# Scale of the first norm from small TensorE products with the weight blocks as stationary operand, loaded in blocks of 128 columns

## Chip, cores and metric

The kernel runs on one core of one Trainium2 chip. The metric is the device time of one execution in microseconds (us); the median of the runs is compared. Before the change three runs took 1184.43, 1188.86 and 1189.87 us, median 1188.86.

## What is computed

One decoder layer on 1024 tokens of width 1024, in float32. What matters here is the first line of the layer: a norm whose scale and shift come from a vector `c`.

```python
c_act = jax.nn.silu(c)
mod = c_act @ w_mod[l] + b_mod[l]
sh1, sc1, g1, sh2, sc2, g2 = jnp.split(mod[:, None, :], N_MOD, axis=-1)
h = rms_norm(x, norm_mix_w[l]) * (1.0 + sc1) + sh1
proj = h @ w_in[l]
```

`w_mod` is 1024 x 6144, so `sc1` alone is the product of a vector with a 1024 x 1024 matrix of 4 MB. After `proj` come a gated recurrence and a gated delta rule (which inverts triangular 128 x 128 blocks), an output projection, and a multi-layer perceptron with a norm of the same kind.

## The kernel before, in words

**Recorder and planner.** The body does not issue instructions. `Proxy` and `Queue` objects stand for the engines (PE is TensorE, V or DVE VectorE, A or ACT ScalarE, G or POOL GpSimd, SP the DMA queue) and record each operation with a modelled length. `Recorder.schedule` (lines 176 to 319) then runs a greedy list schedule over the engines and `emit` (line 321) issues the operations in that order from line 329, which is why nearly every row of the profile reads L329. Each engine then works through its own list strictly in that order. The planner's numbers are at the top: `LAT` (lines 40 to 42), `COLD` (before that time TensorE operations are counted twice, line 286), and the length of a DMA, bytes over 358 per ns (line 408). Operations recorded with `rec.bb` are TensorE's backbone; others are fitted around it.

**The beginning.** `x` comes as eight tiles `xt` of 128 tokens. `xnorm(t)` squares one on ScalarE, takes the reciprocal root on GpSimd (`rs`) and scales it on VectorE (tile 3 on ScalarE). `xhalf(hf, k)` transposes four 128 x 128 blocks on TensorE into one PSUM tile `xTp`, and makes from it the high part `hh` (ScalarE) and the remainder `hl` (VectorE) of the normed and scaled activations, both multiplied by column `k` of `A1`, the scale. `hf` 0 covers tokens 0 to 511, `hf` 1 the others. So nothing can be projected before `A1`.

**A1 before.** The weights of `sc1` come in eight loads `sc1_w`, four for columns 0 to 511 and four for 512 to 1023, in runs of 512 columns (2 KB). `sc1_part` (line 704) adds the eight row blocks, each times its element of `cact` (the column of silu(c)), into `sc1_acc`: blocks 1, 3 and 5 of each half are multiplied on ScalarE and added on GpSimd (`SC1_POOL`), the others go through VectorE. Four products with a column of ones (`sc1_c`, line 722) sum over the partitions, and two VectorE operations make four columns of `A1`.

**After A1.** `Proj.split` (line 642) splits a 1024 x 128 block of `w_in` into `wh` (ScalarE) and `wl` (GpSimd). `Proj.third(i)` multiplies a third of the tokens: 8 blocks by 3 matmuls of 342 columns into `p`. The order on TensorE is the first third of `k0`, of `ab` (`ab_third`, 16 matmuls) and of `k1` (lines 745 to 748), the transposes of `hf` 1, the second thirds, then the column sums `sh_c` of the shift (`sh1_acc`, lines 752 to 757, added up from eight 512 KB loads `sh1_w`), which everything after needs as two further columns of `hh` and `hl`; then `ab`'s last third. From it follow `gcs`, `gT`, a round trip to DRAM (`gdr`, `k_gb`), the decay `k_dm`, and for each of four heads `key(h)`: `ktok`, `kk`, `LT`. When `LT` of all four is there, `inverse` (line 887) does a long VectorE recurrence (`ftmp`, `xx`) and the TensorE products `ie`, `ig`, `ih`, `ix`. TensorE works on `z`, `q` and `v` projections beside it.

**Loads.** All DMAs go through one queue, SP, in its order: `c`, x0, x1, three small ones, x2, x3, four `sc1_w`, the block of `w_in` for `k0`, `wab`, four `sc1_w`, x4, x5, the block for `k1`, x6, x7, two small ones, eight `sh1_w`, eight small rows. Each waits for the landing of the one eight places before it. The eight small rows end in `rows_ps`, a transposition on TensorE (line 741).

Of the kernel before, what the change touches and what calls it, by code (L numbers as in the profile page):

```python
# [10 lines left out]
F32 = mybir.dt.float32  # L11
F32R = mybir.dt.float32r
AF = mybir.ActivationFunctionType
ALU = mybir.AluOpType
# [5 lines left out]
P = 128  # L20
T = 1024
D = 1024
NK = 8
# [8 lines left out]
COL_X, COL_Y, COL_Q, COL_K, COL_V, COL_Z, COL_AB = 0, 512, 1024, 1536, 2048, 2560, 3072  # L32
# [7 lines left out]
LAT = {("PE", "DVE"): 0.2, ("PE", "ACT"): 0.2, ("ACT", "DVE"): 0.04, ("DVE", "ACT"): 0.04, ("ACT", "POOL"): 0.08,  # L40
       ("DVE", "POOL"): 0.08, ("POOL", "DVE"): 0.04, ("POOL", "ACT"): 0.04, ("DVE", "PE"): 0.06, ("ACT", "PE"): 0.06,
       ("POOL", "PE"): 0.06, ("DVE", "DVE"): 0.04, ("ACT", "ACT"): 0.04, ("POOL", "POOL"): 0.05, ("PE", "PE"): 0.0}
SC1_EARLY = 4
SC1_POOL = (1, 3, 5)
COLD = 30.0
SIDE_SCALE = 1.4
TINY_RUN, TINY_SHARE = 0.2, 1.0
SLACK, SLACK_TINY = 0.3, 2.0
# [78 lines left out]
class Recorder:  # L127
# [48 lines left out]
    def schedule(self):  # L176
# [34 lines left out]
        while done < len(ops):  # L211
# [72 lines left out]
            else:  # L284
                t = max(t, port) if op.port else t
                now[e] = fin = t + op.dur * (2 if e == "PE" and t < COLD else 1)
                port = max(port, fin) if op.port else port
# [51 lines left out]
class Proxy:  # L339
# [5 lines left out]
    def __getattr__(self, name):  # L345
        fn = getattr(self.nce, name)

        def call(*a, **k):
            isap = lambda v: isinstance(v, (View, bass.AP))
            outs = [v for n, v in k.items() if n in ("out", "accum_out") and isap(v)]  # L350
            rest = list(a)
            if "out" not in k:
                outs.append(rest.pop(0))
            ins = [v for v in rest if isap(v)] + [v for n, v in k.items() if n not in ("out", "accum_out") and isap(v)]
            self.rec.add(self.eng, fn, a, k, outs, ins, self.length(name, outs[0], ins, k), self.port(name, outs[0], ins))
            return None
        return call
# [39 lines left out]
class Queue(Proxy):  # L397


    def __getattr__(self, name):  # L400
        fn = getattr(self.nce, name)

        def call(out, in_):
            n = 4
            big_ = out if isinstance(out, View) else in_
            for d in big_.shape:
                n *= d
            self.rec.add("SP", fn, (), {"out": out, "in_": in_}, [out], [in_], 0.05 + n / 358e3)
            self.rec.ops[-1].load = isinstance(out, View)
        return call  # L410

# [2 lines left out]
def hybrid_body(ctx, tc, x, c, norm_mix_w, norm_mlp_w, w_mod, b_mod, w_in,  # L414
# [3 lines left out]
                w_out, w_up, w_down, final_norm_w, out, dbg=None):  # L418
    nc = tc.nc
    rec = Recorder(nc)  # L420
    PE, V, A, G = (Proxy(rec, n, e) for n, e in (("PE", nc.tensor), ("DVE", nc.vector), ("ACT", nc.scalar), ("POOL", nc.gpsimd)))
    SP = Queue(rec, "SP", nc.sync)
# [16 lines left out]
    def buf(pool, tag, bufs, shape, dt, name):  # L439
        key = (tuple(shape), dt)  # L440
        if key not in protos:
            protos[key] = dp.tile(list(shape), dt, tag=f"proto{len(protos)}", name=f"proto{len(protos)}")
        b = Buf(pool, tag, bufs, tuple(shape), dt, name, protos[key])
        return View(b, protos[key])

    def big(name, dt=F32, n=1024):
        return buf(bp, "b", N_B, [P, n], dt, name)
# [7 lines left out]
    def ps(name):  # L455
        return buf(pp, "ps", N_PS, [P, 512], F32, name)

    def small(name, n, dt=F32):
        return buf(cp, name, 1, [P, n], dt, name)

    def v3(ap, n=128):
        return ap.rearrange("p (a b) -> p a b", b=n)
# [8 lines left out]
    def mm(o, lhsT, rhs, start=True, stop=True, **kw):  # L471
        PE.matmul(o, lhsT, rhs, start=start, stop=stop, **kw)

    def tr(o, in_, idn):
        PE.transpose(o, in_, idn)
# [11 lines left out]
    ones = small("ones", P)  # L487
# [15 lines left out]
    ccol, cth, cact = small("ccol", 8), small("cth", 8), small("cact", 8)  # L503
# [15 lines left out]
    bcol = small("bcol", 64)  # L519
# [25 lines left out]
    wm_r = w_mod.rearrange("a (k p) n -> (a k) p n", p=P)  # L545
    halves = [slice(0, 512), slice(512, 1024)]

    def macc(acc, wt, k, spread=False):
        if k == 0:
            if spread:  # L550
                A.mul(acc, wt, cact[:, 0:1])
            else:
                V.tensor_scalar(acc, wt, cact[:, 0:1], None, op0=ALU.mult)
        elif spread:
            A.mul(wt, wt, cact[:, k:k + 1])
            G.tensor_tensor(out=acc, in0=acc, in1=wt, op=ALU.add)
        else:
            V.scalar_tensor_tensor(out=acc, in0=wt, scalar=cact[:, k:k + 1], in1=acc, op0=ALU.mult, op1=ALU.add)

# [2 lines left out]
    def load_w(c0, name):  # L562
        w = big(f"{name}_w")
        SP.dma_start(out=v3(w), in_=wr_[:, :, c0:c0 + P])
        return w
# [13 lines left out]
    sc1_w, sh1_w = {}, {}  # L579
    wm_p = w_mod.rearrange("a (k p) n -> (a p) k n", p=P)  # L580
    rec.early = True
    for t in range(4):
        SP.dma_start(out=xt[t], in_=xs[t])
        if t == 1:
            SP.dma_start(out=rows2[0:48, :], in_=b_mod.rearrange("a (r p) -> (a r) p", p=P))
            SP.dma_start(out=rows2[48:56, :], in_=norm_mix_w.rearrange("a (r p) -> (a r) p", p=P))
            SP.dma_start(out=rows2[56:64, :], in_=norm_mlp_w.rearrange("a (r p) -> (a r) p", p=P))
    for n in range(4):
        sc1_w[n] = big(f"sc1_w{n}")
        SP.dma_start(out=v3(sc1_w[n], 512), in_=wm_p[:, 2 * n:2 * n + 2, D:D + 512])  # L590
    wk0 = load_w(COL_K, "k0")
    wab = big("wab")[:, 0:64].rearrange("p (k j) -> p k j", j=8)
    SP.dma_start(out=wab, in_=wr_[:, :, COL_AB:COL_AB + 8])
    for n in range(4):
        sc1_w[4 + n] = big(f"sc1_w{4 + n}")
        SP.dma_start(out=v3(sc1_w[4 + n], 512), in_=wm_p[:, 2 * n:2 * n + 2, D + 512:2 * D])
    for t in range(4, NT):
        if t == 6:
            wk1 = load_w(COL_K + P, "k1")
        SP.dma_start(out=xt[t], in_=xs[t])  # L600
    rec.early = False

# [4 lines left out]
    A1 = small("A1", NK)  # L607
# [28 lines left out]
    class Proj:  # L636
# [2 lines left out]
            self.b = None  # L639
            self.p = {}  # L640

        def split(self):
            raw = self.raw or load_w(self.c0, self.name)
            self.w = (big(f"{self.name}_wh", F32R), big(f"{self.name}_wl", F32R))
            A.copy(self.w[0], raw)
            G.tensor_tensor(out=self.w[1], in0=raw, in1=self.w[0].bitcast(F32), op=ALU.subtract)

        def third(self, i):
            self.p[i] = p = ps(f"{self.name}_p{i}")
# [18 lines left out]
    projs = [Proj(COL_K, "k0", True, wk0), Proj(COL_K + P, "k1", True, wk1)]  # L668
# [17 lines left out]
    def xhalf(hf, k):  # L686
        px = ps(f"xTp{k}_{hf}")
        for j in range(4):
            tr(px[:, j * P:(j + 1) * P], xt[4 * hf + j][:, k * P:(k + 1) * P], ident)
        a, b = hT[k]  # L690
        s = halves[hf]
        A.activation(a[:, s], px, AF.Identity, scale=A1[:, k:k + 1])
        V.scalar_tensor_tensor(out=b[:, s], in0=px, scalar=A1[:, k:k + 1], in1=a[:, s].bitcast(F32),
                               op0=ALU.mult, op1=ALU.subtract)
# [4 lines left out]
    pt = ps("rows2_ps")  # L699
    tr(pt[:, 0:64], rows2, ident[:64, :64])  # L700
    V.tensor_copy(bcol, pt[:, 0:64])
    sc1_acc = big("sc1_acc")

    def sc1_part(hf, ks):
        acc = sc1_acc[:, halves[hf]]
        wts = [sc1_w[4 * hf + k // 2][:, halves[k % 2]] for k in range(NK)]
        for k in ks:
            if k in SC1_POOL:
                A.mul(wts[k], wts[k], cact[:, k:k + 1])
                if k != SC1_POOL[0]:  # L710
                    G.tensor_tensor(out=wts[SC1_POOL[0]], in0=wts[SC1_POOL[0]], in1=wts[k], op=ALU.add)
            else:
                macc(acc, wts[k], k)
        if 7 in ks and SC1_POOL:
            V.tensor_tensor(out=acc, in0=acc, in1=wts[SC1_POOL[0]], op=ALU.add)

    sc1_part(0, range(8))
    for hf in range(2):
        pc = ps(f"sc1_c{hf}")
        ks = slice(4 * hf, 4 * hf + 4)  # L720
        for k in range(4):
            mm(pc[:, 4 * hf + k:4 * hf + k + 1], sc1_acc[:, (4 * hf + k) * P:(4 * hf + k + 1) * P], ones[:, 0:1])
        V.tensor_tensor(out=A1[:, ks], in0=pc[:, ks], in1=bcol[:, 8 + ks.start:8 + ks.stop], op=ALU.add)
        V.scalar_tensor_tensor(out=A1[:, ks], in0=A1[:, ks], scalar=1.0, in1=bcol[:, 48 + ks.start:48 + ks.stop],
                               op0=ALU.add, op1=ALU.mult)
        if hf == 0:
            projs[0].split()
            sc1_part(1, range(SC1_EARLY))
        for k in range(4 * hf, 4 * hf + 4):
            xhalf(0, k)  # L730
        if hf == 0:
            sc1_part(1, range(SC1_EARLY, 8))
    for t in range(4, NT):
        xnorm(t)
    for k in range(NK):
# [8 lines left out]
    rec.bb = True  # L744
    projs[0].third(0)
    ab_third(0)
    projs[1].split()
    projs[1].third(0)
    rec.bb = False
    for k in range(NK):  # L750
        xhalf(1, k)
    sh1_acc = big("sh1_acc")
    for k in range(NK):
        macc(sh1_acc, sh1_w[k], k, k < 3)
    psh = ps("sh1_c")
    for k in range(NK):
        mm(psh[:, k:k + 1], sh1_acc[:, k * P:(k + 1) * P], ones[:, 0:1])
# [28 lines left out]
    for t in range(NT):  # L786
# [7 lines left out]
                    in1=dtb[:, None, :].to_broadcast([P, 8, 4]), op=ALU.add)  # L794
# [137 lines left out]
    def mod_part(vec, name, acc, k):  # L932
        wt = big(f"{name}_w{k}")
        SP.dma_start(out=wt, in_=wm_r[k, :, vec * D:(vec + 1) * D])
        macc(acc, wt, k, k == 0)

    def mod_sum(vec, name):
        acc = big(f"{name}_acc")
# [355 lines left out]
    for t in range(NT):  # L1294
        for i in range(2):
            gemm_o(lcat, lw, t, i, f"wl{t}{i}",
                   lambda p, s: V.scalar_tensor_tensor(out=x1[t][:, s], in0=p, scalar=rsl[:, t:t + 1], in1=x1[t][:, s],
                                                       op0=ALU.mult, op1=ALU.add))
# [300 lines left out]
```

## Time and profile before

| what | value |
|---|---|
| runs | 1184.43, 1188.86, 1189.87 us, median 1188.86 |
| the profiled execution: its own time | 1189.07 us |
| its span, first to last instruction | 1187.2 us |
| TensorE busy in the span | 1142.0 us, 96% |
| VectorE, ScalarE, GpSimd busy | 857.9, 617.3, 385.8 us |
| mean granted TensorE clock | 0.980 of full speed |
| moved by DMA | 229.52 MB, 193 GB/s over the span |

A row of a timeline reads: start, length, engine, operation, what it writes and reads, count, and in brackets how long its engine was idle before and what ended that. PEld is TensorE's loading of the stationary operand, PE its matmuls. A chain of waits is followed back from the last instruction: each row is the work, or the wait, that held up what comes next. A table by stretches gives for each stretch the busy time of every engine, the granted clock, and the DMA's busy share and rate. The granted clock is shown as 1.00 until the first change of it in an execution.

### The profile page before, as it was taken

How to read it: one execution, taken by the hardware profiler on the slowest of the kernel's cores; microseconds unless marked ns; L12 is line 12 of the kernel's file. 1: busy time of each engine (PE TensorE's matmuls, PEld its weight loads, DVE VectorE, ACT ScalarE, POOL GpSimd, SP SyncE). 2: the span in 40 equal slices, each digit the busy share in tenths (PEclk: the TensorE clock that was granted, in tenths of full speed). 3: DMA queues.
4: the chain of work that ended last, by engine and by line, in shares of the span. 5: the costliest groups of instructions: out<-in, count | busy, mean ns of one | idle time of the engine just before them, and what ended most of it. 6: DMA issues, size and time to landing. Idle time of an engine off the chain costs nothing.

```text
span 1187.2 us, 15989 instructions
## 1 busy us (share of the span) xinstructions
PE 1142.0 (96%) x5936; PEld 989.2 (83%) x5936; DVE 857.9 (72%) x1125; ACT 617.3 (52%) x990; POOL 385.8 (32%) x229
## 2 busy tenths in 40 slices
PE   3999899999999999999999999999999999999997
PEld 3889899999999997877888888888788888888885
DVE  6968696698987899977966666656775578775553
ACT  6547317435453868367665555555655524443341
POOL 4708620335242563400001121121430076822130
PEclk7899998999989999999999999999999999999999
DMA  9622430623651635323067777866899848855531
GB/s 338 206 74 101 147 124 19 212 72 115 224 195 54 199 124 210 107 107 107 36 231 256 246 264 241 273 230 235 302 401 387 314 160 312 302 206 188 197 147 71
DMA packets 127151, 229.52 MB, mean 193 GB/s; under 512 B 10657, under 2 KB 51806, under 8 KB 127074
## 3 DMA queue, kind: packets, MB, share of 16 engines
q1 hardware_dynamic: 127074, 228.51, 55.8%
q8 instruction: 46, 0.75, 0.3%
q14 instruction: 31, 0.25, 0.1%
HBM read 171.83 MB, written 56.65 MB: 192 GB/s over the span
## 4 chain that ended last, share of the span: by engine, by line
PE 84%; DVE 7%; issue 3%; ACT 2%; POOL 1%; DMA 1%; SPq 1%; POOLq 0%; DVEq 0%; ACTq 0%
PE dn L329 26%; PE upx L329 15%; PE upz L329 7%; PE k_p L329 4%; PE wg L329 4%; PE upy L329 4%; PE lx_p L329 3%; PE v_p L329 3%; PE ly_p L329 3%; PE wl L329 3%; PE q_p L329 2%; PE ch L329 2%; DVE xx L329 1%; DVE ftmp L329 1%; DMA x<-in_x_dram 1%
## 5 line engine op out<-in xcount | busy, mean ns | idle before, releaser
L329 PE MATMUL upx<-h2h,U 128*128 128x512 f32 x512 | 167.8, 394 | 0.0
L329 POOL TENSOR_TENSOR wd<-wd,wd 128x512 f32<-128x512 f32 x32 | 44.7, 1400 | 231.3 <-DMA wd<-in_w_down_dram 214.4
L329 PEld LDWEIGHTS upx<-h2h,U 128*128 128x128 f32 x512 | 96.1, 188 | 22.7 <-issue 0.2
L329 PE MATMUL upx<-h2l,U 128*128 128x512 f32 x256 | 100.9, 394 | 0.0
L329 ACT ACTIVATE act<-act 128x512 f32<-128x512 f32 x112 | 70.6, 633 | 38.6 <-DVE act L329 37.2
L329 DVE TENSOR_TENSOR U<-wu,U 128x512 fp32r<-128x512 f32 x112 | 76.7, 704 | 16.6 <-ACT U L329 16.5
L329 PE MATMUL upz<-h2h,U 128*128 128x512 f32 x256 | 85.0, 394 | 0.0
L329 ACT CAST U<-wu 128x512 fp32r<-128x512 f32 x112 | 67.2, 618 | 18.4 <-DVE wu L329 9.1
L329 DVE TENSOR_TENSOR act<-upz,ek 128x512 f32<-128x512 f32 x32 | 22.1, 691 | 60.3 <-PE upz L329 44.9
L329 ACT COPY ek<-upx 128x512 f32<-128x512 f32 x48 | 28.1, 586 | 59.7 <-PE upx L329 59.5
L329 PEld LDWEIGHTS upx<-h2l,U 128*128 128x128 f32 x256 | 48.1, 188 | 11.4
L329 PEld LDWEIGHTS upz<-h2h,U 128*128 128x128 f32 x256 | 48.1, 188 | 11.2
L329 POOL TENSOR_TENSOR xb<-xb,keep 128x512 f32<-128x512 f32 x8 | 13.5, 1696 | 122.8 <-DVE keep L329 122.8
L329 PE MATMUL upz<-h2l,U 128*128 128x512 f32 x128 | 50.3, 393 | 0.0
L329 PE MATMUL upy<-h2h,U 128*128 128x512 f32 x128 | 42.7, 394 | 0.0
L329 ACT ACTIVATE vn<-ch,bcoef 128x128 f32<-128x128 f32 x32 | 11.6, 367 | 57.0 <-PE ch L329 57.0
L329 POOL TENSOR_TENSOR ssq<-ssq,mhalf 128x1 f32<-128x1 f32 x16 | 11.7, 732 | 90.0 <-DVE ssq L329 89.9
L329 PE MATMUL k_p<-hh,k_wh 128*128 128x342 f32 x96 | 32.3, 337 | 5.0 <-DVE hl L329 3.9
L329 PE MATMUL z_p<-hh,z_wl 128*128 128x342 f32 x96 | 31.5, 328 | 3.2 <-POOL z_wl L329 3.2
L329 PE MATMUL k_p<-hl,k_wh 128*128 128x342 f32 x96 | 32.7, 341 | 0.0
L329 DVE TENSOR_TENSOR wu<-wu,wu 128x512 f32<-128x512 f32 x48 | 32.6, 683 | 0.0
L329 PE MATMUL k_p<-hh,k_wl 128*128 128x342 f32 x96 | 32.2, 335 | 0.0
(572 smaller groups left out, 3788.2 us busy)
## 6 DMA issues: line engine op xcount, KB each, us to landing
L<-aod SPq DMA_DIRECT2D x56, 512.0 KB, 4.7
R<-in_w_down_dram SPq DMA_DIRECT2D x40, 512.0 KB, 6.6
wu<-in_w_up_dram SPq DMA_DIRECT2D x32, 512.0 KB, 4.2
aod<-as SPq DMA_DIRECT2D x64, 256.0 KB, 3.0
wd<-in_w_down_dram SPq DMA_DIRECT2D x32, 512.0 KB, 7.2
aod<-act SPq DMA_DIRECT2D x48, 256.0 KB, 2.6
x<-in_x_dram SPq DMA_DIRECT2D x16, 512.0 KB, 4.8
sc_w<-in_w_mod_dram SPq DMA_DIRECT2D x16, 512.0 KB, 5.8
```

The costliest lines, as they stand in the source:

```text
L329: op.fn(*[res(v) for v in op.a], **{n: res(v) for n, v in op.k.items()})
```

## The change

`sc1` is made wholly on TensorE. Its weights are loaded in eight blocks of 128 columns, `sc1_w[j]`, each with all eight row blocks; their runs are 512 bytes. For each `j` eight products accumulate one column in PSUM: the stationary operand is a 128 x 128 block of weights, the moving one a single column of `cact`. One VectorE operation turns it into a column of `A1`, with the bias and the norm's weight folded into `B1` ahead of it, and `xhalf(0, j)` follows at once. The multiplications and additions of `sc1_part` are gone from VectorE, ScalarE and GpSimd. The first two weight splits go from GpSimd to VectorE. In the loads, the block for `k1` and `wab` move ahead of x4. The sum of `sh1` loses its GpSimd share: one multiplication on ScalarE, seven operations on VectorE. Two numbers of the planner change, and with them its order everywhere.

```diff
-SC1_EARLY = 4
-SC1_POOL = (1, 3, 5)
-COLD = 30.0
+COLD = 11.0
...
-            self.rec.add("SP", fn, (), {"out": out, "in_": in_}, [out], [in_], 0.05 + n / 358e3)
+            self.rec.add("SP", fn, (), {"out": out, "in_": in_}, [out], [in_], 0.05 + n / 390e3)
...
-    for n in range(4):
-        sc1_w[n] = big(f"sc1_w{n}")
-        SP.dma_start(out=v3(sc1_w[n], 512), in_=wm_p[:, 2 * n:2 * n + 2, D:D + 512])
+    def load_sc1(j):
+        sc1_w[j] = v3(big(f"sc1_w{j}"))
+        SP.dma_start(out=sc1_w[j], in_=wm_p[:, :, D + j * P:D + (j + 1) * P])
+
+    for j in range(4):
+        load_sc1(j)
     wk0 = load_w(COL_K, "k0")
+    for j in range(4, NK):
+        load_sc1(j)
+    wk1 = load_w(COL_K + P, "k1")
     wab = big("wab")[:, 0:64].rearrange("p (k j) -> p k j", j=8)
     SP.dma_start(out=wab, in_=wr_[:, :, COL_AB:COL_AB + 8])
-    for n in range(4):
-        sc1_w[4 + n] = big(f"sc1_w{4 + n}")
-        SP.dma_start(out=v3(sc1_w[4 + n], 512), in_=wm_p[:, 2 * n:2 * n + 2, D + 512:2 * D])
     for t in range(4, NT):
-        if t == 6:
-            wk1 = load_w(COL_K + P, "k1")
         SP.dma_start(out=xt[t], in_=xs[t])
...
-        def split(self):
+        def split(self, e=G):
...
-            G.tensor_tensor(out=self.w[1], in0=raw, in1=self.w[0].bitcast(F32), op=ALU.subtract)
+            e.tensor_tensor(out=self.w[1], in0=raw, in1=self.w[0].bitcast(F32), op=ALU.subtract)
...
-    sc1_part(0, range(8))
-    for hf in range(2):
-        pc = ps(f"sc1_c{hf}")
-        ks = slice(4 * hf, 4 * hf + 4)
-        for k in range(4):
-            mm(pc[:, 4 * hf + k:4 * hf + k + 1], sc1_acc[:, (4 * hf + k) * P:(4 * hf + k + 1) * P], ones[:, 0:1])
-        V.tensor_tensor(out=A1[:, ks], in0=pc[:, ks], in1=bcol[:, 8 + ks.start:8 + ks.stop], op=ALU.add)
...
+    B1 = small("B1", NK)
+    V.scalar_tensor_tensor(out=B1, in0=bcol[:, 8:16], scalar=1.0, in1=bcol[:, 48:56], op0=ALU.add, op1=ALU.mult)
+    for j in range(NK):
+        pc1 = ps(f"sc1_c{j}")
+        for k in range(NK):
+            mm(pc1[:, 0:1], sc1_w[j][:, k, :], cact[:, k:k + 1], k == 0, k == NK - 1)
+        V.tensor_scalar(A1[:, j:j + 1], pc1[:, 0:1], bcol[:, 48 + j:49 + j], B1[:, j:j + 1], op0=ALU.mult, op1=ALU.add)
+        xhalf(0, j)
+        if j == 3:
+            projs[0].split(V)
...
-    projs[1].split()
+    projs[1].split(V)
...
-        macc(sh1_acc, sh1_w[k], k, k < 3)
+        macc(sh1_acc, sh1_w[k], k)
```

The first place is TensorE's list at the third and fourth tile of `x`. `xTp2_0_196<-ident_72,x2_118` is a transposition of a block of the third tile; before, the twelve of the two tiles stand together ahead of the first column sums:

```order
L329 MATMUL xTp3_0_195<-ident_72,x2_118 128x128
L329 MATMUL xTp4_0_197<-ident_72,x2_118 128x128
L329 MATMUL xTp5_0_199<-ident_72,x2_118 128x128
L329 MATMUL xTp0_0_186<-ident_72,x3_120 128x128
L329 MATMUL xTp1_0_190<-ident_72,x3_120 128x128
L329 MATMUL xTp2_0_192<-ident_72,x3_120 128x128
L329 MATMUL xTp3_0_195<-ident_72,x3_120 128x128
L329 MATMUL xTp4_0_197<-ident_72,x3_120 128x128
L329 MATMUL xTp5_0_199<-ident_72,x3_120 128x128
L329 MATMUL sc1_c0_260<-ones_114,sc1_acc_216 128x1 x4
```

After it, at the same place, the products of the first two weight blocks (`sc1_w0`, `sc1_w1`) stand between the transpositions:

```order
L327 MATMUL xTp4_0_201<-ident_72,x1_110 128x128
L327 MATMUL sc1_c0_217<-cact_168,sc1_w0_124 128x1
L327 MATMUL xTp5_0_203<-ident_72,x1_110 128x128
L327 MATMUL xTp0_0_190<-ident_72,x2_118 128x128
L327 MATMUL sc1_c0_217<-cact_168,sc1_w0_124 128x1
L327 MATMUL xTp1_0_194<-ident_72,x2_118 128x128
L327 MATMUL sc1_c1_226<-cact_168,sc1_w1_126 128x1
L327 MATMUL sc1_c0_217<-cact_168,sc1_w0_124 128x1
L327 MATMUL xTp2_0_196<-ident_72,x2_118 128x128
L327 MATMUL sc1_c1_226<-cact_168,sc1_w1_126 128x1
```

The transpositions of the third tile now wait in the list behind products, and so behind the landing of the first two blocks. The list holds 11 transpositions ahead of the first product, 21 more up to the last, and 32 behind it.

The second place is the end of the products on TensorE, at the first third of `k0`. After the change (before, the first third of `k0` follows eight transpositions behind the four column sums above):

```order
L327 MATMUL xTp7_0_360<-ident_72,x3_122 128x128
L327 MATMUL sc1_c7_348<-cact_168,sc1_w7_144 128x1
L327 MATMUL k0_p0_384<-hh0_252,k0_wh_262 128x342
L327 MATMUL k0_p0_384<-hl0_264,k0_wh_262 128x342
L327 MATMUL sc1_c7_348<-cact_168,sc1_w7_144 128x1
L327 MATMUL k0_p0_384<-hh0_252,k0_wl_273 128x342
L327 MATMUL k0_p0_384<-hh1_271,k0_wh_262 128x342
L327 MATMUL sc1_c7_348<-cact_168,sc1_w7_144 128x1
L327 MATMUL k0_p0_384<-hl1_284,k0_wh_262 128x342
L327 MATMUL k0_p0_384<-hh1_271,k0_wl_273 128x342
```

The first projection matmul now stands behind 60 of the 64 products, and 8 projection matmuls stand ahead of the last product.

The third place is TensorE's list ahead of the inverse (`ie`). Before, the last of the third `v0_p2` stand there, 20 of them behind `q0_p1`:

```order
L329 MATMUL v0_p2_1781<-hl5_390,v0_wh_1551 128x342
L329 MATMUL v0_p2_1781<-hh5_372,v0_wl_1565 128x342
L329 MATMUL v0_p2_1781<-hh6_375,v0_wh_1551 128x342
L329 MATMUL v0_p2_1781<-hl6_401,v0_wh_1551 128x342
L329 MATMUL ie0_1811<-xn0_828,LT_1128 128x128 x4
```

After it the `ie` products follow `q0_p1` directly:

```order
L327 MATMUL q0_p1_1792<-hl6_391,q0_wh_1521 128x342
L327 MATMUL q0_p1_1792<-hh6_379,q0_wl_1534 128x342
L327 MATMUL q0_p1_1792<-hh7_414,q0_wh_1521 128x342
L327 MATMUL q0_p1_1792<-hl7_430,q0_wh_1521 128x342
L327 MATMUL q0_p1_1792<-hh7_414,q0_wl_1534 128x342
L327 MATMUL ie0_1831<-xn0_1168,LT_1172 128x128 x4
```

All matmuls of `v0` now stand behind the inverse. Between `sh_c` and `gT` there stand 64 projection matmuls before and 72 after; `ktok` of the last head stands behind 84 `z` matmuls before and behind 74 after.

More of the change, by code (lines that the diff above doesn't have):

```diff
@@ L546, in hybrid_body, with macc @@
     halves = [slice(0, 512), slice(512, 1024)]
-    def macc(acc, wt, k, spread=False):
+    def macc(acc, wt, k):
         if k == 0:
[L550 to L556, printed above, removed]
+            A.mul(acc, wt, cact[:, 0:1])
         else:
@@ L701, in hybrid_body @@
     V.tensor_copy(bcol, pt[:, 0:64])
[L702 to L715, printed above, removed]
-    sc1_part(0, range(8))
-    for hf in range(2):
-        pc = ps(f"sc1_c{hf}")
-        ks = slice(4 * hf, 4 * hf + 4)
-        for k in range(4):
-            mm(pc[:, 4 * hf + k:4 * hf + k + 1], sc1_acc[:, (4 * hf + k) * P:(4 * hf + k + 1) * P], ones[:, 0:1])
-        V.tensor_tensor(out=A1[:, ks], in0=pc[:, ks], in1=bcol[:, 8 + ks.start:8 + ks.stop], op=ALU.add)
[L724 to L732, printed above, removed]
+    B1 = small("B1", NK)
[8 more added lines that the diff above has]
+            projs[0].split(V)
     for t in range(4, NT):
@@ L934, in mod_part @@
         SP.dma_start(out=wt, in_=wm_r[k, :, vec * D:(vec + 1) * D])
-        macc(acc, wt, k, k == 0)
+        macc(acc, wt, k)
     def mod_sum(vec, name):
```

## Prediction

> **What bounds the kernel now.** The page first: its span, the busy shares, TensorE and its clock in 40 slices of 29.7 us.
>
> ```profile
> span 1187.2 us, 15989 instructions
> PE 1142.0 (96%) x5936; PEld 989.2 (83%) x5936; DVE 857.9 (72%) x1125; ACT 617.3 (52%) x990; POOL 385.8 (32%) x229
> PE   3999899999999999999999999999999999999997
> PEclk7899998999989999999999999999999999999999
> ```
>
> TensorE bounds everything but the first slice, where it is 30% busy, and the clock is among its lowest in the first two (7 and 8 tenths). What can be won or lost lies there, so I read next the chain of waits up to the inverse (start, length, what). Its rows on TensorE carry my prices.
>
> ```profile
> 33.01 2.84 DVE x L329
> ...
> 38.08 0.64 PE xTp L329 x3
> 38.72 0.86 PE k_p L329 x3
> ...
> 42.17 0.08 PE rows_ps L329
> ...
> 43.36 0.44 PE xTp L329 x4
> ...
> 46.87 6.75 PE k_p L329 x43
> 53.61 2.48 PE ab L329 x16
> 56.09 3.78 PE k_p L329 x24
> 59.87 1.91 PE sh_c L329 x16
> ...
> 78.21 0.11 PE gT L329
> ```
>
> Up to 35.85 us the chain is the norm of the later tiles (`x`), not `sc1`; then it is TensorE alone to `sh_c` at 59.87. TensorE has two prices: a transposition 0.64/3 = 0.213 us at 38.1 and 0.44/4 = 0.11 at 43.4; a projection matmul 0.86/3 = 0.287, then 6.75/43 = 0.157; an `ab` matmul 2.48/16 = 0.155. The table by stretches shows why. I cut it where the clock changes, which is at steps of 3.41 us (columns: stretch, length, busy and count by engine, granted clock, DMA).
>
> ```profile
> core 0: us, PE busy (x) PEld busy (x) DVE busy (x) ACT busy (x) POOL busy (x), PEclk, DMA share, GB/s
> 7.34:10.75 3.41, 3.09 (x13) 2.40 (x14) 2.21 (x8) 2.58 (x6) 1.14 (x3) 1.00 1.03 398
> 10.75:14.16 3.41, 1.67 (x12) 1.20 (x12) 1.78 (x3) 2.88 (x4) 1.54 (x2) 1.00 1.06 378
> 34.66:38.06 3.40, 2.17 (x9) 2.11 (x10) 3.40 (x5) 2.64 (x4) 3.40 (x3) 0.50 1.03 412
> 38.08:41.47 3.39, 3.39 (x15) 3.27 (x15) 3.39 (x4) 0.00 (x0) 3.25 (x2) 0.50 0.26 86
> 58.55:61.95 3.40, 3.21 (x25) 2.89 (x23) 1.38 (x4) 0.00 (x0) 0.85 (x1) 1.00 0.03 5
> 61.97:65.37 3.40, 3.12 (x12) 1.64 (x13) 1.76 (x19) 0.95 (x9) 0.00 (x0) 0.50 0.00 0
> ```
>
> 38.08 to 41.47 is full of matmuls at clock 0.50, and they run fast from its end. The row 58.55 to 61.95 matters most here: TensorE is 3.21 of 3.40 us busy, but 1.91 us of that are the one-column products `sh_c`, and the clock of the next row is 0.50. So one-column products keep TensorE busy and do not hold its clock.
>
> **What the change adds on TensorE.** 64 products; eight column sums of the same shape make 16 records in the chain (`sh_c`), two each, so 128. Their prices: 1.91/16 = 0.119 us with the clock up (row 59.87), and cold, from the loading of the weights, 1.78/8 = 0.223 us:
>
> ```profile
> 18.16 1.78 PEld L329 LDWEIGHTS sc_c<-ones,sc_acc 128*128 128x128 f32 x8 [4.85 <-DVE sc_acc L329]
> ```
>
> So 15.2 us warm or 28.5 us cold, less the 16 records of `sc_c` that go (1.9 to 3.6). They start when the first block of weights has landed. Before, the first load is there when ScalarE starts on it at 10.50. The new loads have runs of 512 bytes; the block for `k1` has such runs at 24.5 to 25.5 us, the first `sc1` loads have 2 KB at 11 to 13 us (last column GB/s):
>
> ```profile
> 10.50 0.73 ACT L329 ACTIVATE sc_w<-sc_w,cact 128x512 f32<-128x512 f32 x1 [0.27 <-DMA sc_w<-in_w_mod_dram]
> 11.00:13.00 2.00, 0.88 (x8) 0.64 (x7) 0.78 (x2) 1.76 (x3) 0.43 (x1) 1.00 1.05 389
> 24.50:25.50 1.00, 0.00 (x0) 0.00 (x0) 1.00 (x3) 0.79 (x3) 0.55 (x1) 0.50 1.18 306
> ```
>
> 524 KB take 1.35 us at 389 and 1.71 at 306 GB/s: 0.37 more per load. The first block lands at 10.9 and all that follows the eight loads is 3.0 us later; bounds 0 and 3.0. The Trainium skill, "DMA: Bandwidth & Descriptors", table of specifications, gives 512 bytes as the least transfer for line rate, by which the first block would land 0.4 us earlier and the later loads 3.0. The 306 GB/s beside 389 speak against it.
>
> Between the first product and the last, TensorE's list holds 21 transpositions and 8 projection matmuls. Nothing there holds the clock: two to three transpositions fall on each 3.4 us, and 2.17 us of transpositions and matmuls in the row 34.66 to 38.06 did not raise it. So the stretch is cold: 28.5 + 21 x 0.213 + 8 x 0.287 = 35.3 us, and 0.2 for waits: the last product ends at 46.4. Then one to two stretches of 3.4 us pass before the clock is up; I take 5.1 us (bounds 3.4 and 6.8, or about 0.8 us on the sum each way), in which 16 projection matmuls and 2 transpositions run: 51.5. The rest is 72 projection matmuls at 0.157 = 11.3, 30 transpositions at 0.11 = 3.3 and 32 `ab` at 0.155 = 5.0, together 19.6, so `sh_c` starts at 71.1 in place of 59.87: **+11.2 us**. Nothing else is late by then: the tiles are normed at 35.85 (row 33.01) and the loads behind the products, 3.0 us later, feed matmuls that stand after 46.4.
>
> **What the change takes away** gives nothing by that sum. The additions of `sc1`, on VectorE and GpSimd:
>
> ```profile
> L329 DVE SCALAR_TENSOR_TENSOR sc_acc<-sc_w,cact,sc_acc 128x512 f32<-128x512 f32 x8 | 8.9, 1114 | 2.2 <-DMA sc_w<-in_w_mod_dram 2.1
> ```
> ```profile
> L329 POOL TENSOR_TENSOR sc_w<-sc_w,sc_w 128x512 f32<-128x512 f32 x4 | 6.3, 1586 | 2.1 <-ACT sc_w L329 1.9
> L329 POOL TENSOR_TENSOR k_wl<-k_w,k_wh 128x1024 fp32r<-128x1024 f32 x4 | 10.7, 2668 | 5.4 <-ACT k_wh L329 5.4
> ```
>
> VectorE loses 8.9 us of additions, gains two splits (below the 2.67 each that GpSimd took) and more of the sum of `sh1`. That sum ended here, 59.7 us:
>
> ```profile
> 58.41 1.28 DVE L329 SCALAR_TENSOR_TENSOR sh_acc<-sh_w,cact,sh_acc 128x1024 f32<-128x1024 f32 x1
> ```
>
> GpSimd's two parts of it come to VectorE at about 2 us each, and its loads come 3.0 later: about 67, still hidden behind TensorE until 71.1. If the products were warm it would be uncovered by a few us.
>
> **Behind `sh_c`.** 72 projection matmuls instead of 64 stand ahead of `gT`: 8 x 0.157 = +1.3 us. The chain into the inverse starts from `gT`, since GpSimd waits for its round trip, and TensorE's waits before the inverse are short:
>
> ```profile
> POOL k_dm L329 <- DMA k_gb<-gdr: 27.7, 1, 27.7
> ```
> ```profile
> PE ie L329 <- ACT xn L329: 4.1, 1, 4.1
> PE z_p L329 <- POOL z_wl L329: 3.2, 1, 3.2
> PE ktok L329 <- DVE k2T L329: 2.0, 1, 2.0
> ```
>
> The 20 matmuls of `v0` that stood ahead of `ie` no longer cover that wait: 20 x 0.157 = +3.1. `ktok` of the last head stands behind 10 fewer `z` matmuls; the 2.0 us of wait may go, and the 3.2 of `z_wl` too, as GpSimd has less to do. From +1.3 + 3.1 = +4.4 down to +4.4 - 5.2 = -0.8; I take +2.4, the one small wait gone. The profiled execution took 1189.07 us (0.2 over the median, 1.9 over its span): 1189.07 + 11.2 + 2.4 = **1202.7 us**, 1.2% above the median of 1188.86. A measurement of this kernel can tell about 0.5%, 5.9 us, from no change.
>
> **Rivals.** *B, the clock stays up through the products* (0.22; the other side, no slower). If a busy TensorE is all the clock asks for, the products, gapless from 10.9, cost 15.2 us, the 21 transpositions 2.3 and the 8 matmuls 1.3: the last ends at 29.7. Then the small rows decide: `rows_ps` at 42.17 waits for loads that now come 3.0 later,
>
> ```profile
> 39.98 0.22 SPq L329 DMA_DIRECT2D rows<-in_gdn_norm_w_dram  x1
> ```
>
> so 45.2, and after it 9 transpositions, 54 projection and 16 `ab` matmuls: 1.0 + 8.5 + 2.5 = 12.0, `sh_c` at 57.2, -2.7 us, and with +2.4 behind it 1188.8. With the loads at the old rate 1185.8, and with -0.8 behind it 1182.6, the best I can work out. It decides if clock 1.00 outlasts the products. The Trainium skill, "TensorE: Matmul & The Clock Gate", section "Why this matters for your kernels", asks for no idle gaps over about 3 us to avoid a drop: by that rule the sum is this rival's 1188.8, by the row 58.55 to 61.95 it is my 1202.7. The trace disagrees with the rule there (no such gap, and 0.50 behind it).
>
> *C, the first stretches stay warm* (0.12). Before, 13 instructions in 7.34 to 10.75 raised the clock, and 12 in the next held it one stretch longer. After, 11 transpositions (11 x 0.213 = 2.3 us) stand ahead of the products. If that is enough, the clock is up from 10.75 to 17.6, about 58 products at 0.119 in place of 0.223, and 1202.7 - 6.5 = 1196.2. Against it: in 34.66 to 38.06 2.17 us were too little.
>
> *D, the waits behind absorb it* (0.09). TensorE's three waits are 9.3 us in sum; were they slack that the delay eats, 1202.7 - 9.3 = 1193.4. Against it: their chain starts at `gT`, which moves with `sh_c`.
>
> That the change does not do what it says can be left out: the products stand in TensorE's list, the additions are gone from the others.
>
> **How the numbers follow.** My case has 0.57. It and C lie over 0.5% up (0.69); D lies at that bound, 0.04 above and 0.05 within; B is split, 0.13 within and 0.09 faster. Slower 0.73, same 0.18, faster 0.09. My case spans 1198.7 to 1205.5: the work behind at -0.8 or +4.4 in place of +2.4, and 0.8 each way for the end of the cold stretch. Another 3.4 us without the clock costs up to 1.6 more (12 matmuls at 0.287 instead of 0.157): high end 1207. Down, C and D belong in the range and the upper part of B, without its fastest: low end 1187.
>
> **What would show it.** Right: granted clock 0.50 from about 11 to 50 us with TensorE gapless; a product record at 0.22 us; `sh_c` at about 71, `gT` at about 91, `ie` near 195, TensorE's wait ahead of `ie` above 4.1 us; nothing else changed by more than a few us. The clock step fails if the row of the products shows 1.00 or a record takes 0.12; then `sh_c` starts at or before 60 and TensorE idles ahead of `rows_ps`. The step on the work behind fails if `ie` comes much later or earlier after `gT` than 101.7 us (179.93 - 78.21):
>
> ```profile
> 179.93 7.95 PE ie L329 x48
> ```

## The result and the profile after

| | before | after |
|---|---|---|
| median of the runs | 1186.81 us (6 runs, 1184.01 to 1191.6) | 1203.42 us (6 runs, 1200.45 to 1205.27) |
| the profiled execution: time, span | 1189.07, 1187.2 us | 1202.87, 1200.8 us |
| TensorE busy, idle in the span | 1142.0, 45.2 us | 1165.5, 35.3 us |

The ratio is 1.0133, with a 95% interval of 1.0103 to 1.0163: the change made the kernel 1.3% slower. 1202.7 us were forecast. The total agrees; three of the steps behind it do not, as will be seen.

The page of the changed kernel, the same lines as before:

```profile
span 1200.8 us, 16217 instructions
...
PE 1165.5 (97%) x6048; PEld 1012.1 (84%) x6048; DVE 827.4 (69%) x1122; ACT 613.0 (51%) x982; POOL 360.2 (30%) x221
...
PE   7989899999999999999999999999999999999997
...
PEclk9989999999999999999999999999999999999999
```

TensorE's first slice went from 3 to 7 tenths. Over the whole span TensorE has 23.5 us more to do (1165.5 - 1142.0) and idles 9.9 us less (45.2 - 35.3), which makes the 13.6 us of the span. This sum, work plus idle time of the engine that bounds the kernel, is the safest way to read everything below. (The profiled execution of before lies 2.3 us over its median, so the spans are 13.6 us apart and the medians 16.6.) The first 50 us by stretch, of before and of after:

```profile
0.00:50.00 50.00, 28.93 (x150) 25.19 (x151) 38.17 (x63) 33.36 (x50) 27.91 (x27) 0.80 0.90 314
```
```profile
0.00:50.00 50.00, 41.97 (x204) 40.47 (x205) 18.27 (x49) 19.80 (x31) 6.88 (x17) 1.00 0.90 286
```

Here TensorE's busy time (third number) rises by 13.0 us, so 13.0 us of the new work lie where it idled before, and 10.5 do not. VectorE, ScalarE and GpSimd lose 19.9, 13.6 and 21.0 us in this stretch. Over the whole span they lose 30.5, 4.3 and 25.6, so what ScalarE does not do here it mostly does later, and none of it made the kernel shorter.

Now the chain of waits of the changed kernel, at the places that the prediction spoke of:

```profile
20.38 12.59 PE sc_c L327 x60
...
44.43 1.06 PE k_p L327 x3
...
48.29 0.95 PE k_p L327 x6
...
60.82 2.07 DVE sh_acc L327
62.89 2.28 DVE nlam L327
65.17 0.07 DVE sh_acc L327
...
70.80 1.19 DVE sh_acc L327
...
72.14 3.56 PE sh_c L327 x16
...
93.97 0.11 PE gT L327
```

A product's record takes 12.59/60 = 0.210 us, the cold price. The projection matmuls are cold at 44.4 and at 0.95/6 = 0.158 us from 46.4 on. Then there is something new: between 52 and 72 us the chain runs over VectorE, and the 16 records of `sh_c` take 3.56 us instead of 1.91. The waits of TensorE name it, and the table by stretches shows the clock that goes with it:

```profile
PE sh_c L327 <- DVE lsp L327: 4.1, 1, 4.1
```
```profile
14.17:17.57 3.40, 3.40 (x19) 3.40 (x19) 0.00 (x0) 0.00 (x0) 0.00 (x0) 1.00 1.20 290
...
61.95:65.36 3.41, 3.41 (x24) 2.60 (x23) 3.41 (x3) 0.20 (x1) 3.41 (x2) 1.00 0.00 0
...
68.78:72.18 3.40, 0.04 (x1) 0.07 (x1) 3.40 (x5) 0.08 (x1) 2.00 (x1) 0.75 0.57 154
72.19:75.60 3.41, 3.41 (x16) 3.40 (x16) 1.39 (x11) 0.12 (x1) 0.00 (x0) 0.50 0.02 5
```

TensorE has nothing to do from 68.0 to 72.1, its clock falls in that gap, and `sh_c` runs at 0.50. The row 14.17 to 17.57 has a trap: the granted clock stands at 1.00 in the middle of the cold products, since the column shows 1.00 until the first fall of the clock, here at about 70.5 us (0.75 in the row 68.78 to 72.18). Where the column has not changed yet, the price of a known instruction tells the clock, not the column.

### The profile page after: what moved, and what is told of

It is laid out like the page before. It is cut to its first block, busy times and chain, and to the rows that moved or that the text cites. A ratio compares the mean times of both kernels' runs of the same rounds, so it can differ in the third digit from the quotient of the medians.

```text
span 1200.8 us, 16217 instructions
## 1 busy us (share of the span) xinstructions
PE 1165.5 (97%) x6048; PEld 1012.1 (84%) x6048; DVE 827.4 (69%) x1122; ACT 613.0 (51%) x982; POOL 360.2 (30%) x221
## 4 chain that ended last, share of the span: by engine, by line
PE 86%; DVE 6%; ACT 3%; issue 2%; DMA 1%; POOL 1%; POOLq 0%; SPq 0%; DVEq 0%; ACTq 0%
PE dn L327 26%; PE upx L327 15%; PE upz L327 7%; PE lx_p L327 4%; PE wg L327 4%; PE upy L327 3%; PE q_p L327 3%; PE v_p L327 3%; PE ly_p L327 3%; PE z_p L327 3%; PE wl L327 3%; PE k_p L327 2%; PE sc_c L327 2%; PE ch L327 1%; PE cho L327 1%
## 5 line engine op out<-in xcount | busy, mean ns | idle before, releaser
L327 PEld LDWEIGHTS upx<-h2l,U 128*128 128x128 f32 x256 | 48.1, 188 | 11.3
L327 ACT COPY ek<-upx 128x512 f32<-128x512 f32 x48 | 28.1, 585 | 46.4 <-PE upx L327 45.3
L327 PE MATMUL lx_p<-hh,lx_wl 128*128 128x342 f32 x96 | 31.9, 333 | 0.0
L327 PE MATMUL lx_p<-hh,lx_wh 128*128 128x342 f32 x96 | 31.9, 332 | 0.0
```

Source lines behind the costliest of these rows:

```text
L327: op.fn(*[res(v) for v in op.a], **{n: res(v) for n, v in op.k.items()})
```

## The experiments

Theory 1 is the prediction's: one-column products keep TensorE busy without raising its clock, and their cold records are the cost. Against it stand: the 0.21 us are the price of loading a weight block, whatever moves (2); the sum of the shift on VectorE sets the time (3); the planner's new order further down does (4). The table has all runs (busy and idle are TensorE's, in the profiled execution's span; `sh_c` is its start there; each ratio is to the runs of before that were made beside it):

| kernel | median us | ratio to before (95%) | busy | idle | `sh_c` |
|---|---|---|---|---|---|
| before | 1186.8 | 1 | 1142.0 | 45.2 | 59.8 |
| after | 1203.4 | 1.0133 (1.0103 to 1.0163) | 1165.5 | 35.3 | 72.1 |
| 128-column products | 1196.2 | 1.0081 (1.0058 to 1.0103) | 1154.1 | 40.8 | 65.9 |
| one product of eight | 1194.4 | 1.0069 (1.0044 to 1.0094) | 1149.5 | 44.1 | 64.2 |
| both old planner numbers | 1194.2 | 1.0064 (1.0039 to 1.0089) | 1161.6 | 31.4 | 67.5 |
| GpSimd part of the shift back | 1195.5 | 1.0077 (1.0054 to 1.0099) | 1160.6 | 31.9 | 71.8 |
| 128 columns + both old numbers | 1192.8 | 1.0045 (1.0028 to 1.0061) | 1152.1 | 37.1 | 65.0 |
| cold time 30 alone | 1192.5 | 1.0045 (1.0028 to 1.0062) | 1160.6 | 30.3 | 67.7 |
| DMA rate 358 alone | 1194.4 | 1.0061 (1.0046 to 1.0077) | 1161.8 | 31.0 | 72.5 |
| cold time 12 | 1199.7 | 1.0106 (1.0085 to 1.0126) | 1163.5 | 34.8 | 74.6 |
| four more splits on VectorE | 1194.8 | 1.0067 (1.0046 to 1.0089) | 1158.5 | 30.2 | 66.5 |
| 128 columns + cold time 30 + the splits | 1189.4 | 1.0020 (1.0009 to 1.0032) | 1149.0 | 38.2 | 62.0 |
| before + the new planner numbers | 1188.9 | 1.0014 (1.0002 to 1.0027) | 1138.4 | 47.9 | 62.3 |
| before + first two splits on VectorE | 1188.5 | 1.0021 (1.0008 to 1.0034) | 1141.6 | 44.1 | 60.7 |

**The products with 128 columns.** The only edit; the order on every engine stays as it is:

```diff
-            mm(pc1[:, 0:1], sc1_w[j][:, k, :], cact[:, k:k + 1], k == 0, k == NK - 1)
+            mm(pc1[:, 0:P], sc1_w[j][:, k, :], cact[:, k:k + 1].to_broadcast([P, P]), k == 0, k == NK - 1)
```

> The moving column of each of the 64 products is repeated to 128 columns (the same sum, written 128 times; column 0 is used). The order on every engine is that of the changed kernel. Theory 1 (one-column products keep TensorE busy but do not raise its clock, and the cold records are the cost): the transpositions and the wide products raise the clock by about 14 to 18 us, a record then takes 0.11 instead of 0.21 us, the last product ends at 28 to 33 us instead of 44.4, the column sums sh_c start at 58 to 65 instead of 72.1, and the time is 1190 to 1196 us. Rival 2 (0.21 us is the price of loading a new fp32 weight block here, whatever moves through it): records stay at 0.21 us or get longer, the last product ends at 44 us or later, the time is 1203 us or more.

The timeline of TensorE in this kernel (start, length, what, count):

```profile
14.60 1.06 PE L327 MATMUL sc_c<-cact,sc_w 128*128 128x128 f32 x4
...
16.67 0.61 PE L327 MATMUL sc_c<-cact,sc_w 128*128 128x128 f32 x4
...
18.89 7.40 PE L327 MATMUL sc_c<-cact,sc_w 128*128 128x128 f32 x60
...
32.27 0.39 PE L327 MATMUL sc_c<-cact,sc_w 128*128 128x128 f32 x2
```

From about 16 us four records take 0.61 instead of 1.06 us, and 60 take 7.40: the clock is up. The last product ends at 32.7 instead of 44.4, with 128 times as many columns moved. That settles theory 1 against 2: what was cold was the clock, and in this order 128 moving columns raised it where one did not. A transposition, which also moves 128 columns, had the same price as a one-column product all along (0.213 and 0.223 us cold, 0.11 and 0.119 warm), so the wider product costs nothing more of its own. The Trainium skill, "TensorE: Matmul & The Clock Gate", section "Why this matters for your kernels", asks for no idle gaps over about 3 us, to avoid a drop. As a rule that would be enough for the full clock, it does not agree with these two traces: the narrow and the wide products stand in the same order, TensorE waits there no longer than 0.8 and 1.1 us at a time, and only the wide ones ran at the full clock.

Of the 12 us gained at the products, 6.2 reach `sh_c` and 7.2 the end. TensorE now starves before it, as its waits show:

```profile
PE rows_ps L327 <- DMA rows<-in_gdn_norm_w_dram: 4.6, 1, 4.6
...
PE sh_c L327 <- DVE lsp L327: 2.9, 1, 2.9
```

The small rows are the bound that the prediction's rival B named (45.2 there; `rows_ps` stands at 48.2). `sh_c` at 65.9 and 1196.2 us lie just outside the ranges of theory 1, for the wait for VectorE that it did not have.

**One product of eight.**

```diff
-            mm(pc1[:, 0:1], sc1_w[j][:, k, :], cact[:, k:k + 1], k == 0, k == NK - 1)
+            if k == 0:
+                mm(pc1[:, 0:1], sc1_w[j][:, k, :], cact[:, k:k + 1], True, True)
```

> Leaves out seven of the eight products of each column of the scale (one row block of eight is summed); the loads stay, the planner reorders around the shorter products. Theory 1: 112 records of 0.21 us go, 23.5 us of TensorE; the small rows and VectorE's sum of the shift end last instead, sh_c starts at 57 to 64 us, the time is 1187 to 1195 us. Rival 3 (the sum of the shift, now wholly on VectorE and GpSimd-disturbed, sets the start of sh_c by itself): sh_c still starts at 70 us or later and the time stays at 1200 us or more. Rival 4 (the planner's new order further down is the cost): 1200 us or more as well, with sh_c early.

`sh_c` starts at 64.2, just over the 57 to 64 of theory 1, and the time is 1194.4 us, within its range. Rival 3 falls as the sole cause. Rival 4 is not decided by this run, since the planner makes a new order around the shorter products, and new orders alone gained as much in runs below. And with nearly no products left the kernel is still 0.7% slower than before: some 7.5 us of the 16.6 are not those products.

**The planner's numbers.** First both put back, then each alone, a control one unit off, and the new numbers in the kernel before:

```diff
-COLD = 11.0
+COLD = 30.0
...
-            self.rec.add("SP", fn, (), {"out": out, "in_": in_}, [out], [in_], 0.05 + n / 390e3)
+            self.rec.add("SP", fn, (), {"out": out, "in_": in_}, [out], [in_], 0.05 + n / 358e3)
```

> Only the two numbers of the planner are put back (cold until 30.0, DMA at 358). Theory 1: the products are the same and as cold, so the last ends at 43 to 46 us and the time is within 4 us of the changed kernel's 1203. Rival 4 (the planner's order is the cost): at least 6 us faster, 1197 us or less.

> The changed kernel with only the planner's cold time put back to 30.0 (DMA still at 390). If the planner's order is bad because it takes the cold products at half their price from 11 us on, this alone brings it back: 1192 to 1197 us. If the DMA number is what matters: 1201 us or more.

> The changed kernel with only the planner's DMA rate put back to 358 (cold time still 11.0). The counterpart: 1201 us or more if the cold time is the cost, 1192 to 1197 us if the DMA rate is. If both single numbers give 1192 to 1197, it is no particular number: any new order is better than this one, and the 9 us are the chance of one greedy order.

The control is the line `COLD = 12.0` alone:

> A control of the planner: the cold time at 12.0 instead of 11.0, which changes nothing that the kernel computes and makes another order from the first products on. If the changed kernel's order is one unlucky draw of the greedy planner: 1192 to 1198 us, as with the other new orders. If an early cold time as such is bad: 1200 us or more.

> The kernel before with the planner's two new numbers only (cold 11.0, DMA 390), products, loads and splits as before. If the numbers cost by themselves: 6 us or more over the kernel before, 1193 us or more. If they cost only where the products are cold and mispriced: within 3 us of the kernel before.

1194.2, 1192.5 and 1194.4 us: theory 1's 4 us were wrong in the first of these, and each single number brings the same 9 to 11 us, which is the third outcome named for the DMA rate. In the kernel before the new numbers cost 0.14%, near nothing. The control came out between its two cases, at 1199.7, with an interval that overlaps the changed kernel's. So the changed kernel's order is a bad one by 3.7 to 10.9 us, part of it the luck of a greedy order, as one unit of the cold time seems to be worth 3.7. Which rule of the planner makes the two orders with an early cold time and the fast DMA the worst is not settled. One difference goes with it: 18 or 19 matmuls of `v0` stand ahead of `ie` in the three orders with an old number, none in the changed kernel and 4 in the control. But 4 stand there too in the run below with GpSimd's part put back (1195.5 us), so this is not shown to be the cause.

Two of these runs also say what the delay at the start is worth. `gT`, from which the chain into the inverse starts, in the kernel with the cold time at 30 and in that with the DMA rate at 358 (count, min/median/max ns, first and last start):

```profile
L327 PE MATMUL gT<-ident,gcs x1: 272/272/272, 85.4 to 85.4; 128*32 128x128 f32 x1
```
```profile
L327 PE MATMUL gT<-ident,gcs x1: 273/273/273, 93.2 to 93.2; 128*32 128x128 f32 x1
```

It starts 7.8 us later in the second, and the second takes 1.9 us longer. In the second `sh_c` and `gT` stand where they stand in the changed kernel (72.5 and 93.2 against 72.1 and 93.97), and it is 9 us faster. In these orders a late chain into the inverse is mostly absorbed, since TensorE has other projections to do; what counts is how long it works and how often it waits. From 100 to 200 us the kernel with the DMA rate at 358 idles 4.2 us (the changed kernel 4.9) and the one before 9.3. First the kernel with 358, then the one before:

```profile
100.00:150.00 50.00, 47.14 (x320) 46.56 (x319) 41.30 (x53) 29.75 (x67) 41.42 (x32) 1.00 0.46 152
150.00:200.00 50.00, 48.65 (x339) 48.37 (x338) 42.01 (x93) 21.98 (x47) 8.55 (x7) 1.00 0.30 96
```
```profile
100.00:150.00 50.00, 44.81 (x296) 44.18 (x295) 37.67 (x58) 24.42 (x48) 33.92 (x34) 0.97 0.39 127
150.00:200.00 50.00, 45.89 (x323) 45.62 (x323) 41.45 (x84) 21.41 (x45) 6.69 (x3) 0.93 0.23 74
```

**GpSimd's part of the shift's sum put back.**

```diff
-        macc(sh1_acc, sh1_w[k], k)
+        macc(sh1_acc, sh1_w[k], k, k < 3)
```

(with the lines of `macc` that multiply on ScalarE and add on GpSimd.)

> The sum of the shift gets its GpSimd part back (blocks 1 and 2 multiplied on ScalarE, added on GpSimd). Theory 1 with the late sum as a second term: TensorE was done with its projections at 68.0 us, waited 4.1 us for VectorE and then ran sh_c cold (3.54 instead of 1.91 us); with the wait gone sh_c starts at about 68 to 69 us with the clock up and the time is 1196 to 1199 us. If VectorE's sum is late because GpSimd works beside it (a 128x4 operation took 2.36 us there), more work for GpSimd does not help: sh_c at 71 us or later and 1201 us or more.

`sh_c` stayed at 71.8 us, TensorE waited 3.4 us for it: giving VectorE less of the sum did not help. The time fell to 1195.5, lower than theory 1 said, but this is a new order of the planner too, and every new order in these runs was 3.7 us or more faster; this run does not tell the two apart. The next one does for the wait.

**Four more splits on VectorE**, those of `k2`, `k3`, `z0` and the gate weights:

```diff
-            q_.split()
+            q_.split(V if q_.name in ("k2", "k3", "z0") else G)
...
-    G.tensor_tensor(out=gwl, in0=gwt, in1=gwh.bitcast(F32), op=ALU.subtract)
+    V.tensor_tensor(out=gwl, in0=gwt, in1=gwh.bitcast(F32), op=ALU.subtract)
```

> The changed kernel with four more splits (k2, k3, z0 and the gate weights) moved from GpSimd to VectorE; in VectorE's list they stand behind all of the shift's sum. If GpSimd's splits beside it stretch that sum (128x1024 additions of 1.28 us took 2.16 and 3.50, a 128x4 operation 2.36): the last addition ends at 62 to 66 us instead of 71.9, TensorE waits less than 1 us ahead of sh_c, which starts at 66 to 69 us. If VectorE has too much to do by itself: no change, sh_c at 71 us or later. The time: 1191 to 1197 us, since the planner makes a new order too.

VectorE's timeline in the changed kernel and GpSimd's beside it, then the sum's seven additions and `sh_c` in the kernel with the four splits on VectorE:

```profile
58.22 1.28 DVE L327 SCALAR_TENSOR_TENSOR sh_acc<-sh_w,cact,sh_acc 128x1024 f32<-128x1024 f32 x1
...
60.73 2.16 DVE L327 SCALAR_TENSOR_TENSOR sh_acc<-sh_w,cact,sh_acc 128x1024 f32<-128x1024 f32 x1
62.81 2.36 DVE L327 TENSOR_SCALAR nlam<-cols 128x4 f32<-128x4 f32 x1
65.08 3.50 DVE L327 SCALAR_TENSOR_TENSOR sh_acc<-sh_w,cact,sh_acc 128x1024 f32<-128x1024 f32 x1
68.50 2.30 DVE L327 TENSOR_SCALAR lsp<-nlam 128x4 f32<-128x4 f32 x1
```
```profile
59.39 2.42 POOL L327 TENSOR_TENSOR k_wl<-k_w,k_wh 128x1024 fp32r<-128x1024 f32 x1 [10.89 <-ACT k_wh L327]
61.76 3.38 POOL L327 TENSOR_TENSOR gwl<-gwt,gwh 128x1024 fp32r<-128x1024 f32 x1
```
```profile
L327 DVE SCALAR_TENSOR_TENSOR sh_acc<-sh_w,cact,sh_acc x7: 1274/1279/1285, 49.8 to 64.1; 128x1024 f32<-128x1024 f32 x7
...
66.54 1.84 PE L327 MATMUL sh_c<-ones,sh_acc 128*128 128x1 f32 x16
```

In the changed kernel an addition takes 1.28 us up to 59.4, while GpSimd idles, and 2.16 and 3.50 once its splits run. With no split on GpSimd beside the sum (it only sets a few tiles there), every addition takes 1.28 us, the last ends at 65.4, TensorE does not wait, and `sh_c` runs at full clock (1.84 us). VectorE has more to do in this kernel (834.9 us busy against 827.4) and is done with the sum over 6 us earlier: what had held the sum was GpSimd beside it, not the amount of work. The Trainium skill, "SBUF — State Buffer", section "SBUF: two separate sides", has VectorE, in some of its operations, and GpSimd share a port pair that one of them holds for a whole instruction while the other waits; the trace agrees, with two 128x4 operations of 2.36 and 2.30 us beside GpSimd's splits that take 0.17 and 0.16 us here. The median is 1194.8 us, no better than the other new orders (the profiled execution itself took 1190.8).

**The first splits alone, in the kernel before.** `projs[0].split(V)` and `projs[1].split(V)`:

> The kernel before with only the first two splits moved to VectorE, as the change does. Theory 1 gives this part no share in the loss: within 4 us of the kernel before, 1183 to 1191 us.

1188.5 us, 0.2% slower: no gain and hardly a loss.

**What helped, together.** First the wide products with both old numbers, then the wide products with the cold time at 30 and the four splits:

> The 128-column products of the first experiment with the planner's two old numbers of the third (each alone took the changed kernel from 1203 to 1196 and 1194 us). If the cold clock of the products and the planner's order are two separate costs, the gains add: 1203.4 - 7.2 - 9.2 = 1187 us, 1184 to 1190. If both only remove the same wait (the one ahead of sh_c and what follows from it), one hides the other: 1193 to 1196 us.

> Everything that helped together: 128-column products (clock up), the planner's cold time at 30.0, and the four splits on VectorE as in the run beside it. If TensorE's work is what sets the time: it carries 14 us of products, some 12 of them in time in which it idled before, so 1184 to 1190 us, about the kernel before; if the start still waits (small rows, sum of the shift) for over 3 us: 1190 to 1194 us.

The first came out just below the range for two costs of which one hides the other (1193 to 1196), not in that for two that add. It gains only 1.4 us over the numbers alone: TensorE has 9.5 us less to do than with cold products (1152.1 against 1161.6) and idles 5.7 us more. The second is the best form of this change, 1189.4 us, and still 0.20% (0.09 to 0.32) behind the kernel before. In the two profiled executions, whose spans are the same 1187.2 us, it has 7.0 us more work on TensorE than the kernel before (1149.0 against 1142.0) and the same 7.0 less idle time (38.2 against 45.2): the products fill what was idle and no more. TensorE waits there for the first column of `A1` and for the small rows:

```profile
PE rows_ps L327 <- DMA rows<-in_gdn_norm_w_dram: 3.4, 1, 3.4
PE sc_c L327 <- DVE A L327: 3.1, 1, 3.1
```

So of the 16.6 us the wide products alone bring back 7.2, the cold time alone 10.9, and both with the four splits 14.0: the gains overlap and do not add up. No run gives the loads of `sc1` their runs of 2 KB back, so what the slower loads cost by themselves is open.

## Why the prediction was right, and where it was not

**The products are cold: right.** 0.210 us a record (0.223 forecast), 128 of them are 26.9 us (28.5), the last ends at 44.4 (46.4). Widening them, with nothing else changed, took 7.2 us off. The start was right too, 11.3 against 10.9, as was the slower rate of loads in runs of 512 bytes: 290 GB/s in the row 14.17 to 17.57, 306 taken. The row that the step was read from, 58.55 to 61.95, would not have carried it alone. In the kernel before with the first two splits on VectorE, TensorE has the same order there (24 `k_p`, 16 `sh_c`, 16 `ab`), about 1 us later, and the 16 `ab` behind the one-column products take 2.70 us instead of 4.07 at a granted clock of 1.00. What shows the step is the pair with narrow and with wide products.

**The end of the cold stretch: the term was too large.** 5.1 us were taken, with bounds of 3.4 and 6.8; it was 2.0 (46.4 - 44.4). Eight projection matmuls stand between the last products and may have counted towards the rise already; no run tests this. With this, and with the last product out 2.0 us sooner, TensorE was done with its list at 68.0, 3.1 us before the 71.1 forecast.

**"Still hidden behind TensorE": wrong.** The sum of the shift was to end at about 67 and ended at 72. The step added up undisturbed lengths of some 2 us and forgot that GpSimd's splits stand beside them; the trace of before had a 128x4 operation of 2.40 us and an addition of 3.52 at 52 to 58 us that would have said so:

```profile
52.55 2.40 DVE L329 TENSOR_SCALAR nea<-nea 128x4 f32<-128x4 f32 x1
54.87 3.52 DVE L329 SCALAR_TENSOR_TENSOR sh_acc<-sh_w,cact,sh_acc 128x1024 f32<-128x1024 f32 x1
```

It cost a wait of 4.1 us and, as the clock fell in it, 1.6 more in `sh_c`. `sh_c` started at 72.1 against 71.1 because two errors, TensorE's own work 3.1 us too late and the sum's wait of 4.1 left out, nearly cancel: that is luck.

**The work behind `sh_c`: right in size, wrong in its steps.** +2.4 us were forecast. From `sh_c` (+12.3) to the end (+13.6 of the span) it is +1.3. But `ie` starts at 187.4, not near 195, with no wait ahead of it where one above 4.1 was forecast, and 93.4 us behind `gT` where 101.7 was the forecast's own test of this step:

```profile
142.52 33.60 PE z_p L327 x214
176.12 11.29 PE q_p L327 x72
187.40 7.14 PE ie L327 x64
```

The waits of 3.2 and 4.1 us of before are gone, which is rival D's mechanism. The argument against D, that its chain starts at `gT` and moves with `sh_c`, does not hold, as the pair of runs with `gT` 7.8 us apart shows. D gave 1193.4 us, and the orders of the planner with another cold time (30) or DMA rate measured 1192.5 to 1194.4. The changed kernel's own order then lost it again: 20 matmuls of `v0` stand behind `ie`, 20 x 0.157 = 3.1 us, and from 200 to 600 us TensorE idles 10.2 us in short waits against 6.8 before. Together that is 6.5, near the 6.1 by which the delay grows from `ie` (+7.5) to the end (+13.6). The forecast had no term for the quality of an order. So the exactness of the 1202.7 is luck: an absorption and an order's cost were both left out, and `ie` came 7.6 us sooner than forecast while the rest took 7.6 us longer. The part that the runs confirm by itself is the cold products.

**Rivals.** B is refuted as it was put (the records are at 0.21). With the clock up, its 1188.8 was not reached by the wide products alone (1196.2): the wait for VectorE and the planner's order were missing in its sum too. C is refuted by the records at 0.21 from 11.3 us on (its price, 6.5 us, is 6.0 by its own 58 records at 0.223 - 0.119).

## What to carry to other kernels

Work moved to TensorE into time in which it idles was not free here, where it moved one column at a time: it was paid at the cold clock, and so was what stood right behind it. Look whether the same instruction can move a full block for the same price. Count a stretch as hidden only with the neighbours that its engine has there, and take the lengths from rows that have the same neighbours. Where a greedy planner makes the order, compare a change in several orders (a number of the planner one step off), since one order alone was worth up to 11 us here, two thirds of what the change lost.

## What was not expected of the hardware

A one-column fp32 product and one of 128 columns had the same price in these traces, 0.21 us a record cold and 0.12 warm (two records each): nothing is saved by the narrow one. A wait of 4.1 us on TensorE cost more than itself: the clock fell in it, and the next 16 records took 3.56 us instead of 1.91. The 16 `ab` matmuls behind them took 4.72 us, where 16 took 2.48 at full clock; but they took 4.07 in the kernel before too, where no such wait stands ahead of `sh_c`, so only 0.7 us of it is new. And an operation on 128x4 elements took 2.36 us on VectorE because GpSimd was at work beside it.
